# Attention scores and RG-LRU gates on 128 partitions: low parts of keys and gate weights in planes of their own beside zeros

## The chip, the cores and the metric

The kernel runs on one core of one Trainium2 chip. A core has a matrix engine (TensorE, PE in the profile; its weight loads are the rows PEld), a vector engine (VectorE, DVE), a scalar engine (ScalarE, ACT), a general engine (GpSimd, POOL) and an engine that here issues DMAs (SyncE, SP). The metric is the device time of one execution in microseconds (us); lower is better. Before the change the median of three runs is 1901.01 us (1900.91 to 1902.4).

## The reference, cut to what matters

One layer of a hybrid decoder in float32: a SwiGLU feed-forward half step (FFN1), a token mixer, a second feed-forward half step (FFN2). It takes a prompt of 1024 tokens and 8 sequences of 4 sampled tokens, with a model width of 1024. In the mixer two groups run side by side on the same normalised input: a gated linear recurrence (RG-LRU), whose gates come from eight 64 x 64 blocks of weights, and attention over a window of 128 with 8 query heads of 64 on 2 key/value heads.

```python
# RG-LRU gates, xb in 8 blocks of 64 channels
r = sigmoid(einsum('btnc,ncd->btnd', xb, wa) + ba)
i = sigmoid(einsum('btnc,ncd->btnd', xb, wx) + bx)
# attention scores; head size 64, keys: the block of 128 before and its own
s = einsum('...qkgd,...jkd->...kgqj', q, k) * 64 ** -0.5
```

## The kernel before, in words

Features lie on partitions, tokens along the free axis. The tokens are two halves: A has prompt tokens 0 to 511; B has tokens 512 to 1023 and the 32 sampled ones (544 columns, as two products of 272). TensorE goes through FFN1(A), FFN1(B) with the mixer of A between its units, FFN2(A) with the mixer of B, and FFN2(B).

A float32 product is made of float32r products over an exact split of each operand: hi (rounded to float32r) and lo (the rest), as hi.hi + hi.lo + lo.hi. In the main line that is three products for each tile of 128 x 128 weights: `mm3` (L380, lines 381 to 383, 512 columns) for A and `mm3w` (L385, lines 391 and 392, 272 columns) for B.

Where the sum runs over only 64 features, one product takes two of the three parts at a time. The gates (`lru`, L726): of each tile of 128 channels, for each block v of 64, the input's hi lies on the block's 64 partitions and its lo on the other 64 (`ct`, lines 780 to 784). The hi of the gate weights lies on both halves (`lw[:, li, v]`), so one product over 128 partitions (line 791) gives hi.hi and hi.lo. The lo of the weights lies on the block's own 64 partitions of plane 2 of `lw`, and a second product on line 791, over those 64 partitions (`lw[o, li, 2]` and `ct[o]`), adds the third part to the same bank.

The scores (`attn`, L997; one generator for each block of 128 queries and key/value head v) are built alike: `qt` has the queries' hi on the head's own 64 partitions and the lo on the others. `kb`, filled by `keys` (L943), has the keys' hi of each head on both halves (planes 0 and 1) and the lo of both heads in plane 2, each on its own 64 partitions. For each of four queries' tiles one product over 128 partitions (line 1019) is followed by one over 64 (line 1020), both into the same bank; four products make one request to the planner, two requests a block. Scores are 256 columns wide, 128 in the first block of the prompt. The sampled tokens' scores (`attn_s`, L1087) use `mm3` over 128 partitions with the other head's queries set to zero; one of their three stretches of keys takes hi and lo from `kb` (line 1134).

The order of the work is written out by a planner at build time. Every step is a Python generator that asks for an engine with an estimated duration and what it depends on (`Req`); `Sched.run` always emits the instruction that can start first by the estimate. Each engine then executes its instructions in that order, waiting on semaphores. The positions of the mixer's units between those of the FFN stand in `POS`. The charge for four score products is 0.44 us, the charge for a gate product `dP(g, 2)`.

Behind the scores come a masked maximum on DVE (line 1025), the exponential on ACT (line 1037), a division on ACT or DVE (helper `copy`, lines 288 to 292), PE transposes (line 1057), the split of the probabilities (helper `copy` and line 1067) and the products with V (lines 1075, 1076). Other hand-overs to PE: the split of the queries (line 1006) and that of the weight units, which come in by DMA (line 339), go through ACT (line 359) and DVE (line 361) and have three places. `constants` (L660) sets up ones, identity and the like on POOL at the start.

Of the kernel before, what the change touches and what calls it, by code (L numbers as in the profile page):

```python
"""One layer (macaron SwiGLU FFN, RG-LRU + windowed attention mixer, macaron SwiGLU FFN) for a
1024-token prompt and 8 x 4 sampled tokens, run as two halves: tokens 0-511 of the prompt (A), then
tokens 512-1023 with the 32 sampled ones (B). The tensor engine goes through FFN1(A), FFN1(B) with the
mixer of A, FFN2(A) with the mixer of B, FFN2(B).

Features lie on partitions and tokens along the free axis. A float32 product runs as three float32r
passes over exact splits (hi = rounded to float32r, lo = the rest): hi.hi + hi.lo + lo.hi.
"""
# [9 lines left out]
F32 = mybir.dt.float32  # L18
# [7 lines left out]
NB, NT = 8, 4                 # sampled sequences, tokens of each  # L26
T = SEQ + NB * NT             # 1056
HALF = 512                    # prompt tokens of a half
T0, TW = (0, HALF), (HALF, T - HALF)
CB = TW[1] // 2               # columns of a product of B  # L30
# [6 lines left out]
DOWN = {3: 0, **{g[0]: n + 1 for n, g in enumerate(GROUPS[2:])}}     # after which tile of h a group's products come  # L37
NEG = -1e30

# columns of the small per-partition operands  # L40
# [8 lines left out]
N_FFN = 2 * NF + 4 * 5 + 2    # weight units of one FFN  # L49
U_IN = N_FFN                  # k, v, q 0-3, x 0-3, gate 0-3  # L50
# [5 lines left out]
# where the units of the mixer stand between those of the FFN that runs beside it  # L56
POS = ({"k": 19, "v": 21, "q": (5, 5, 27, 28), "x": (6, 8, 12, 24), "g": (28, 30, 33, 36), "o": (47, 48, 48, 49, 49, 49, 50, 52)},
       {"k": 14, "v": 5, "q": (9, 11, 11, 11), "x": (6, 6, 16, 19), "g": (21, 26, 42, 45), "o": (57, 57, 57, 57, 57, 59, 59, 60)})
# of the estimate: reluctance to change the ACT tables, their change, and what an instruction of ACT or DVE has besides its columns
PEN, LOAD, EXTRA = 2.0, 2.6, {"A": 0.12, "D": 0.09}  # L60
WARM = 10                     # products of zeros that raise the tensor engine's clock before the first operands come
ORDER = ((0, 1, 2, 3), (0, 1, 2, 3, "s"))     # of the blocks of attention in A and B; "s": the sampled tokens
MODES = (None, "tanh", "tanh")     # how FFN1(B) and FFN2(A) take silu
MAINCAP = 6                   # banks that products of the main line may hold
DBIAS = 0.8                   # against the vector engine, where the scalar engine can do the same


class Tok:
    """The end of an instruction, by the estimate that orders the emission; None until it is emitted."""
# [6 lines left out]
class Req:  # L76
    __slots__ = ("eng", "dur", "deps", "sets", "when", "lat", "bias")

    def __init__(self, eng, dur, *deps, sets=None, when=None, lat=0.15, bias=0.0):
        self.eng, self.dur, self.deps, self.sets, self.when, self.lat = eng, dur, deps, sets, when, lat  # L80
        self.bias = bias      # against this one of several engines


class Sched:
    """Orders the emission: of all generators' next instructions, the one that can start first."""
# [60 lines left out]
class Banks:  # L146
    """The 8 banks of PSUM, alone or in pairs."""
# [32 lines left out]
class Pool:  # L180
    """Places in an arena, each with the end of its last use."""
# [26 lines left out]
def layer(ctx: ExitStack, tc, t):  # L208
# [15 lines left out]
    kb = const.tile([128, 3, WIN + W], F32R, name="kb")           # hi of each head, lo; the block before the half, then the half  # L224
    vt = const.tile([128, 5, 4, 64], F32R, name="vt")             # the block before the half, then the half; hi and lo of head 0, lo and hi of 1
# [3 lines left out]
    lw = const.tile([128, NLW, 3, 128], F32R, name="lw")          # hi of each block on both halves of the partitions, lo  # L229
    cols = const.tile([128, NCOL], F32, name="cols")  # L230
    ones = const.tile([128, 128], F32R, name="ones")
    bd1 = const.tile([128, 128], F32R, name="bd1")                # ones in each head's block
# [4 lines left out]
    xc3 = const.tile([128, 4, 3], F32, name="xc3")                # the end of A, for B  # L237
# [4 lines left out]
    qss = const.tile([128, 5, 4, 2], F32, name="qss")             # queries' 1 / rms: block (the sampled ones last), head  # L242
# [18 lines left out]
    def P_(b, g):  # L261
        """The product of a half in PSUM: one bank for A, two for B."""
        return ps[:, b:b + 2, :CB] if g else ps[:, b, :]

    def S_(ap, g):
        """A half in SBUF, in the form of P_."""
        return ap.rearrange("p (c n) -> p c n", c=2) if g else ap
# [13 lines left out]
    def dual(n, *deps, psum=False, when=None):  # L281
        """Requests for one pass over n columns on ACT or on DVE."""
        return (Req("A", 0.1 + n * 0.83e-3, *deps, when=when),
                Req("D", 0.07 + n * (1.04e-3 if psum else 0.52e-3), *deps, when=when, bias=DBIAS))

# [13 lines left out]
    tok = Toks()              # named ends: what another generator waits for  # L299
# [4 lines left out]
    def column_sums(lhs, x, g, tk):  # L304
        """lhs (of ones) times x, by x's hi and lo; returns the bank."""
# [16 lines left out]
    order = []                # the units as the main line takes them  # L322
# [3 lines left out]
    FIRST = 2                 # units that come and are split in pieces between the tiles of x; two more wait in the places of B's x  # L326
# [46 lines left out]
    def wait(n, k0):  # L373
        """The weights of unit n from k-tile k0 on."""
        return tok["w", n, k0 * len(pieces_of(n)) // KD]
# [9 lines left out]
    def mm3w(b, g, wh, wl, ah, al, first, last):  # L385
        """The three passes for a half."""
# [9 lines left out]
    def group(n, j, g, srcs, deps):  # L396
        """One [128 features, half] product; srcs: (hi, lo) of the k-tiles; the weights are tile j of unit n."""
# [18 lines left out]
    def abreast(parts):  # L416
        """Products side by side; their results."""
# [33 lines left out]
    def mean_rsqrt(xs, deps, g, n, out, acc, sq, sq2):  # L451
        """out = rsqrt(mean of squares + eps) of the feature tiles xs."""
# [12 lines left out]
    X = [list(range(KD)), list(range(KD, 2 * KD))]        # the places of x  # L465
# [4 lines left out]
    def xsplit(st, name, g):  # L470
        """x with the norm's gain into hi and lo; the products are divided by the rms."""
# [15 lines left out]
    def prenorm(st, name, g):  # L487
        """x / rms with the norm's gain into hi and lo."""
# [22 lines left out]
    def ffn(st, g, st2, u0, mode, rslot=None):  # L511
        """Steps of one FFN on a half: (generator, weight units). mode: "late" divides the products by the rms."""
# [3 lines left out]
        def evg(b, tk, f):  # L516
# [14 lines left out]
            else:             # silu(z) = z (1 + tanh(z / 2)) / 2  # L531
# [49 lines left out]
        def down(gi, m0, mp):  # L581
# [10 lines left out]
            if gi == len(GROUPS) - 1 and m0 == 0:  # L592
                # side by side, while the newest h is still on its way
# [27 lines left out]
    # ================= start =================  # L621
# [7 lines left out]
    def start():  # L629
        """The first loads, in the order in which the products take them."""  # L630
# [29 lines left out]
    def constants():  # L660
# [5 lines left out]
        G.memset(qss, 1.0)  # L666
        yield Req("Q", 0.6, Tok(60.0))
        SP.dma_start(mask, t["mask"])
        # softplus(-lambda), from tanh and the series of atanh
# [42 lines left out]
    # ================= the mixer =================  # L712
# [13 lines left out]
    def lru(i, g, xp):  # L726
# [18 lines left out]
        # convolution  # L745
# [20 lines left out]
        for v in range(2):  # L766
# [6 lines left out]
            V.tensor_tensor(lw[o, li, 2], raw[o], f32(lw[o, li, v]), OP.subtract)  # L773
        # gates: of each block of 64 channels both, from hi and lo on the two halves of the partitions
# [3 lines left out]
        for v in range(2):  # L778
# [10 lines left out]
            for w_, a_, st_ in ((lw[:, li, v], ct, True), (lw[o, li, 2], ct[o], False)):  # L789
                for c in range(1 + g):  # L790
                    PE.matmul(ps[:, b + c, :n], w_, a_[:, c * n:(c + 1) * n], start=st_, stop=not st_)  # L791
# [9 lines left out]
        # a = exp(-8 softplus(-lambda) r); 1 - a^2 = (1 + a^2) tanh(8 softplus(-lambda) r)  # L801
# [9 lines left out]
        # z ** 0.5 = z y, y = z ** -0.5 from exp(-ln(z) / 2) and one step of Newton  # L811
# [17 lines left out]
        if g:  # L829
            # h0 enters the first token of a sampled sequence, whose decay is then cut  # L830
# [60 lines left out]
    def query(b, tk, j, g):  # L891
        """Gain and rotary; the rms divides the scores."""
# [50 lines left out]
    def keys(s, g):  # L943
        """The keys: hi of each head on both halves of the partitions, lo of both heads on their own."""
# [6 lines left out]
        lo = kb[:, 2, WIN:WIN + TW[g]]  # L951
        for v in range(2):
            hi = kb[:, v, WIN:WIN + TW[g]]
# [43 lines left out]
    def attn(g, b, v, ri, Ps, mi):  # L997
# [3 lines left out]
        qt = rm[:, ri, :512]          # hi on the head's own partitions, lo on the others  # L1001
# [5 lines left out]
        whole = g or b                # the block before counts  # L1007
# [5 lines left out]
        kh, kl = kb[:, v, ks], kb[o, 2, ks]  # L1013
        for jj in (0, 2):
            tk = yield Req("P", 0.44, tk, tok["KB", g], banks.soon(), when=banks.has())
            bk = banks.get()
            for j in (jj, jj + 1):
                out = ps[:, bk, (j - jj) * 256 + ko:(j - jj + 1) * 256]
                PE.matmul(out, qt[:, j * 128:j * 128 + 128], kh, start=True, stop=False)  # L1019
                PE.matmul(out, qt[o, j * 128:j * 128 + 128], kl, start=False, stop=True)  # L1020
# [57 lines left out]
        # the parts with lo of V lie on the other partitions  # L1078
# [457 lines left out]
```

## Time and profile before

| what | value |
|---|---|
| median of three runs | 1901.01 us |
| span of the profiled execution, first to last instruction | 1898.9 us |
| granted TensorE clock, mean | 1.000 |
| DVE, ACT busy | 56%, 42% of the span |
| DMA queue q1, share of 16 engines | 29.6% |

The profile has no separate time for the profiled execution beyond its span; the median of the runs lies 2.1 us above that span. A row of a timeline has the start (us from the start of the span), the duration (us), engine, line, operation, the tile written and those read, and sizes: `128*128 128x256` is a product over 128 partitions into 128 rows, with 256 columns moving; `64*128` is one over 64 partitions. `x2` is a merged row of two. A group's row ends with the count, busy time, mean of one (ns), and the idle time ahead of it with what ended it. A row of the waits names who waited for whom, the total (us), how often, and the longest. A row of an instruction by line has minimum, median and maximum of its duration (ns), then first and last start. A row of windows has, for a stretch, its length, then the busy time and instructions of PE, PEld, DVE, ACT and POOL, the granted clock, the DMA share and GB/s. PE products are pipelined, so their rows overlap.

### The profile page before, as it was taken

How to read it: one execution, taken by the hardware profiler on the slowest of the kernel's cores; microseconds unless marked ns; L12 is line 12 of the kernel's file. 1: busy time of each engine (PE TensorE's matmuls, PEld its weight loads, DVE VectorE, ACT ScalarE, POOL GpSimd, SP SyncE). 2: the span in 40 equal slices, each digit the busy share in tenths (PEclk: the TensorE clock that was granted, in tenths of full speed). 3: DMA queues.
4: the chain of work that ended last, by engine and by line, in shares of the span. 5: the costliest groups of instructions: out<-in, count | busy, mean ns of one | idle time of the engine just before them, and what ended most of it. 6: DMA issues, size and time to landing. Idle time of an engine off the chain costs nothing.

```text
span 1898.9 us, 27922 instructions
## 1 busy us (share of the span) xinstructions
PE 1892.9 (100%) x11634; PEld 1702.3 (90%) x11634; DVE 1065.3 (56%) x1638; ACT 790.7 (42%) x1176; POOL 10.3 (1%) x35
## 2 busy tenths in 40 slices
PE   9999999999999999999999999999999999999999
PEld 7888888899999889989988988778889899999999
DVE  6774444476665767646576766766654643233333
ACT  5342222244645466424456566563543322222221
POOL 0000000000000000000000000000000000000000
PEclk9999999999999999999999999999999999999999
DMA  5422223243222212322242322223332322222222
GB/s 168 141 98 92 97 94 117 92 145 99 82 92 96 83 57 74 127 100 87 82 152 94 106 90 78 80 75 103 113 113 90 133 89 89 89 90 90 89 88 82
DMA packets 60253, 187.97 MB, mean 99 GB/s; under 512 B 7376, under 2 KB 9936, under 8 KB 60112
## 3 DMA queue, kind: packets, MB, share of 16 engines
q1 hardware_dynamic: 59984, 186.09, 29.6%
q8 instruction: 91, 1.49, 0.3%
q14 instruction: 34, 0.28, 0.0%
q10 hardware_dynamic: 144, 0.10, 0.0%
HBM read 174.58 MB, written 9.90 MB: 97 GB/s over the span
## 4 chain that ended last, share of the span: by engine, by line
PE 99%; DVE 0%; DMA 0%; ACT 0%; SPq 0%; issue 0%; ACTq 0%
PE ps L391 25%; PE ps L392 24%; PE ps L381 15%; PE ps L382 15%; PE ps L383 15%; PE ps L1020 1%; PE ps L1019 1%; PE ps L1057 1%; PE ps L791 1%; PE ps L1075 0%; PE ps L1076 0%; PE ps L907 0%; PE ps L317 0%; DMA fa<-x 0%; PE ps L1183 0%; DVE fa L556 0%
## 5 line engine op out<-in xcount | busy, mean ns | idle before, releaser
L359 ACT ACTIVATE whi<-raw 128x1024 fp32r<-128x1024 f32 (+1 forms) x312 | 325.2, 1042 | 707.2 <-issue 270.1
L361 DVE TENSOR_TENSOR wlo<-raw,whi 128x1024 fp32r<-128x1024 f32 (+1 forms) x312 | 375.4, 1203 | 195.6 <-ACT whi L359 189.6
L381 PE MATMUL ps<-xh,whi 128*128 128x512 f32 x880 | 350.6, 398 | 0.1
L382 PE MATMUL ps<-xl,whi 128*128 128x512 f32 x880 | 347.6, 395 | 0.3 <-DVE xl L476 0.3
L383 PE MATMUL ps<-xh,wlo 128*128 128x512 f32 x880 | 347.4, 395 | 0.0
L391 PE MATMUL ps<-xh,whi 128*128 128x272 f32 x880 | 256.7, 292 | 0.0
L391 PE MATMUL ps<-xl,whi 128*128 128x272 f32 x880 | 254.0, 289 | 0.0
L392 PE MATMUL ps<-xh,whi 128*128 128x272 f32 x880 | 253.7, 288 | 0.0
L392 PE MATMUL ps<-xl,whi 128*128 128x272 f32 x880 | 253.1, 288 | 0.0
L391 PE MATMUL ps<-xh,wlo 128*128 128x272 f32 x880 | 252.6, 287 | 0.0
L392 PE MATMUL ps<-xh,wlo 128*128 128x272 f32 x880 | 252.6, 287 | 0.0
L556 DVE SCALAR_TENSOR_TENSOR fa<-ps,fa 128x512 f32<-128x512 f32 (+1 forms) x192 | 135.6, 707 | 172.0 <-PE ps L392 103.5
L381 PEld LDWEIGHTS ps<-xh,whi 128*128 128x128 f32 x880 | 165.8, 188 | 38.9 <-ACT xh L474 0.9
L383 PEld LDWEIGHTS ps<-xh,wlo 128*128 128x128 f32 x880 | 165.8, 188 | 38.6
L382 PEld LDWEIGHTS ps<-xl,whi 128*128 128x128 f32 x880 | 165.9, 189 | 37.0 <-DVE xl L476 1.1
L391 PE MATMUL ps<-ha,whi 128*128 128x272 f32 x704 | 191.5, 291 | 0.0
L392 PE MATMUL ps<-ha,whi 128*128 128x272 f32 x704 | 190.8, 288 | 0.0
L391 PEld LDWEIGHTS ps<-xh,whi 128*128 128x128 f32 x880 | 165.4, 188 | 3.5 <-issue 1.5
L392 PEld LDWEIGHTS ps<-xh,whi 128*128 128x128 f32 x880 | 166.3, 189 | 1.3
L392 PEld LDWEIGHTS ps<-xl,whi 128*128 128x128 f32 x880 | 166.5, 189 | 0.0
L391 PEld LDWEIGHTS ps<-xh,wlo 128*128 128x128 f32 x880 | 165.9, 189 | 0.0
L392 PEld LDWEIGHTS ps<-xh,wlo 128*128 128x128 f32 x880 | 165.9, 188 | 0.0
(236 smaller groups left out, 2738.9 us busy)
## 6 DMA issues: line engine op xcount, KB each, us to landing
raw<-w SPq DMA_DIRECT2D x304, 512.0 KB, 3.3
fa<-x SPq DMA_DIRECT2D x8, 272.0 KB, 3.9
xs<-fa SPq DMA_DIRECT2D x8, 272.0 KB, 5.6
fa<-xs SPq DMA_DIRECT2D x8, 272.0 KB, 2.9
y<-fa SPq DMA_DIRECT2D x8, 272.0 KB, 2.0
fa<-x SPq DMA_DIRECT2D x8, 256.0 KB, 4.5
xs<-fa SPq DMA_DIRECT2D x8, 256.0 KB, 4.6
fa<-xs SPq DMA_DIRECT2D x8, 256.0 KB, 3.5
```

The lines of the kernel that those rows point to most:

```text
L359: S.activation(hi, raw, AF.Copy)
L361: V.tensor_tensor(lo, raw, f32(hi), OP.subtract)
L381: PE.matmul(p, wh, ah, start=first, stop=False)
L382: PE.matmul(p, wh, al, start=False, stop=False)
L383: PE.matmul(p, wl, ah, start=False, stop=last)
L391: PE.matmul(ps[:, b, :CB], w, a[:, c0], start=s, stop=e)
L392: PE.matmul(ps[:, b + 1, :CB], w, a[:, c1], start=s, stop=e)
L556: V.scalar_tensor_tensor(x, P_(b, g), fac, x, op0=OP.mult, op1=OP.add)
L791: PE.matmul(ps[:, b + c, :n], w_, a_[:, c * n:(c + 1) * n], start=st_, stop=not st_)
L1019: PE.matmul(out, qt[:, j * 128:j * 128 + 128], kh, start=True, stop=False)
L1020: PE.matmul(out, qt[o, j * 128:j * 128 + 128], kl, start=False, stop=True)
L1057: PE.transpose(ps[:, bk, j * 128:(j + 1) * 128], P[j // 2][:, j % 2, hf * 128:(hf + 1) * 128], ident)
```

## The change

The tile `kb` gets a fourth plane and `lw` too. The lo of head 0's keys stays in plane 2, that of head 1 goes to plane 3; in each plane the other 64 partitions are set to zero once, at the start, by GpSimd. The gate weights' lo of block 0 and 1 lie in planes 2 and 3 of `lw` in the same way. The second product of each pair then runs over all 128 partitions: the lo of the keys or weights meets the hi on its own partitions, and zeros meet the lo on the others. The sampled tokens' scores read plane 2 + v. The program's `dynamic_dma_scratch_size` is set to 1024. The rest of the diff takes out comments.

```diff
-    kb = const.tile([128, 3, WIN + W], F32R, name="kb")
+    kb = const.tile([128, 4, WIN + W], F32R, name="kb")
-    lw = const.tile([128, NLW, 3, 128], F32R, name="lw")
+    lw = const.tile([128, NLW, 4, 128], F32R, name="lw")
...
         G.memset(qss, 1.0)
+        for v in range(2):
+            u = slice(64 - 64 * v, 128 - 64 * v)
+            G.memset(f32(kb[u, 2 + v]), 0.0)
+            G.memset(f32(lw[u, :, 2 + v]), 0.0)
...
-            V.tensor_tensor(lw[o, li, 2], raw[o], f32(lw[o, li, v]), OP.subtract)
+            V.tensor_tensor(lw[o, li, 2 + v], raw[o], f32(lw[o, li, v]), OP.subtract)
...
-            for w_, a_, st_ in ((lw[:, li, v], ct, True), (lw[o, li, 2], ct[o], False)):
+            for w_, st_ in ((lw[:, li, v], True), (lw[:, li, 2 + v], False)):
                 for c in range(1 + g):
-                    PE.matmul(ps[:, b + c, :n], w_, a_[:, c * n:(c + 1) * n], start=st_, stop=not st_)
+                    PE.matmul(ps[:, b + c, :n], w_, ct[:, c * n:(c + 1) * n], start=st_, stop=not st_)
...
-        lo = kb[:, 2, WIN:WIN + TW[g]]
         for v in range(2):
-            hi = kb[:, v, WIN:WIN + TW[g]]
+            hi, lo = kb[:, v, WIN:WIN + TW[g]], kb[:, 2 + v, WIN:WIN + TW[g]]
...
-        kh, kl = kb[:, v, ks], kb[o, 2, ks]
+        kh, kl = kb[:, v, ks], kb[:, 2 + v, ks]
...
-                PE.matmul(out, qt[o, j * 128:j * 128 + 128], kl, start=False, stop=True)
+                PE.matmul(out, qt[:, j * 128:j * 128 + 128], kl, start=False, stop=True)
...
-                kh, kl = (kb[:, v, WIN + HALF:], kb[:, 2, WIN + HALF:]) if h == 2 else (krh, krl)
+                kh, kl = (kb[:, v, WIN + HALF:], kb[:, 2 + v, WIN + HALF:]) if h == 2 else (krh, krl)
...
-    nc = _bacc.Bacc("TRN2", target_bir_lowering=False, num_devices=1)
+    nc = _bacc.Bacc("TRN2", target_bir_lowering=False, num_devices=1, dynamic_dma_scratch_size=1024)
```

## The prediction

> **What bounds the kernel now.** I read four views: the page (engines, chain of waits), the waits of TensorE, the timelines of PE and PEld around one attention block, and the instructions of the lines that the change touches.
>
> ```profile
> span 1898.9 us, 27922 instructions
> PE 1892.9 (100%) x11634; PEld 1702.3 (90%) x11634; DVE 1065.3 (56%) x1638; ACT 790.7 (42%) x1176; POOL 10.3 (1%) x35
> PE 99%; DVE 0%; DMA 0%; ACT 0%; SPq 0%; issue 0%; ACTq 0%
> PE ps L652 <- DVE rm L650: 1.6, 1, 1.6
> PE ps L382 <- DVE xl L476: 0.3, 1, 0.3
> ```
>
> PE is busy for the whole span and is 99% of the chain that ended last. In the whole run it waits 1.9 us for another engine, all of it in the first microseconds. So the time is the sum of what PE's products occupy, and only what shortens PE's own stream counts. But a busy row is not a row at its peak: rows overlap, so the cost of a product is the distance from its start to the start of the next one. That distance must be read from a timeline. Here is PE in one attention block (eight score products), with the main stream before and behind it:
>
> ```profile
> 1204.67 0.39 PE L383 MATMUL ps<-ha,wlo 128*128 128x512 f32 x1
> 1204.90 0.28 PE L1019 MATMUL ps<-kb,rm 128*128 128x256 f32 x1
> 1205.11 0.38 PE L1020 MATMUL ps<-kb,rm 64*128 64x256 f32 x1
> 1205.43 0.38 PE L1019 MATMUL ps<-kb,rm 128*128 128x256 f32 x1
> ...
> 1207.30 0.50 PE L381 MATMUL ps<-ha,whi 128*128 128x512 f32 x1
> 1207.63 0.39 PE L382 MATMUL ps<-ha,whi 128*128 128x512 f32 x1
> ```
>
> In the main stream a 512-column product takes 0.23 us (1204.67 to 1204.90). Inside the block, where products on 128 and on 64 partitions alternate, a 256-column product takes 0.31 us (1205.11 to 1205.43), longer than one with twice the columns. The first product back on 128 partitions, L381 at 1207.30, again takes 0.33. The weight loads (PEld) in the same stretch say why:
>
> ```profile
> 1204.68 0.19 PEld L1019 LDWEIGHTS ps<-kb,rm 128*128 128x128 f32 x1
> 1205.11 0.18 PEld L1020 LDWEIGHTS ps<-kb,rm 64*128 64x128 f32 x1 [0.25 <-issue]
> 1207.30 0.19 PEld L381 LDWEIGHTS ps<-ha,whi 128*128 128x128 f32 x1
> 1207.40 0.19 PEld L382 LDWEIGHTS ps<-ha,whi 128*128 128x128 f32 x1
> ```
>
> The first score's weights load at 1204.68, under the product before it, 0.22 ahead of its own product. L1020's weights start only at 1205.11, together with their product, after PEld had stood 0.25 us with nothing to wait for. The load back to 128 partitions (1207.30) starts with its product too, and the next load follows 0.10 later. [...]
>
> **The change part by part.** It removes the 64-partition form from two places; each instruction there stays, on 128 partitions. The counts:
>
> ```profile
> L1019 PE MATMUL ps<-kb,rm x64: 220/382/388, 642.0 to 1248.4; 128*128 128x256 f32 x56, 128*128 128x128 f32 x8
> L1020 PE MATMUL ps<-kb,rm x64: 322/382/384, 642.1 to 1248.8; 64*128 64x256 f32 x56, 64*128 64x128 f32 x8
> L791 PE MATMUL ps<-rm,lw x48: 282/338/504, 460.9 to 1152.4; 128*128 128x272 f32 x16, 64*128 64x272 f32 x16, 128*128 128x512 f32 x8, 64*128 64x512 f32 x8
> ```
>
> For a 256-column product with its own load among products of full height, the trace has the sampled tokens' products:
>
> ```profile
> 1323.38 0.28 PE L381 MATMUL ps<-rm 128*128 128x256 f32 x1
> 1323.50 0.28 PE L382 MATMUL ps<-rm 128*128 128x256 f32 x1
> 1289.00 0.26 PE L383 MATMUL ps<-kb,rm 128*128 128x32 f32 x1
> 1289.11 0.26 PE L381 MATMUL ps<-kb,rm 128*128 128x32 f32 x1
> ```
>
> So 0.12 us for 256 columns (1323.38 to 1323.50), and 0.11 for a 32-column one, where the load sets the pace; I take 0.11 for 128 columns, between the two.
>
> *Scores, 256 columns.* Before: 1204.90 to 1207.63 is 2.73 us for eight scores and one 512-column product. After: 8 x 0.12 + 0.23 = 1.19. Saved 1.54 a block; 56 pairs at four a block are 14 blocks: **21.6 us**.
>
> *Scores, 128 columns* (the first prompt block, where the block before doesn't count), and the gates:
>
> ```profile
> 641.98 0.22 PE L1019 MATMUL ps<-kb,rm 128*128 128x128 f32 x1
> 644.25 0.39 PE L382 MATMUL ps<-xl,whi 128*128 128x512 f32 x1
> 460.63 0.29 PE L391 MATMUL ps<-xh,wlo 128*128 128x272 f32 x1
> 460.75 0.29 PE L392 MATMUL ps<-xh,wlo 128*128 128x272 f32 x1
> 460.88 0.82 PE L791 MATMUL ps<-rm,lw 128*128 128x512 f32 x2
> 461.86 0.29 PE L392 MATMUL ps<-xh,whi 128*128 128x272 f32 x1
> 1149.58 0.85 PE L791 MATMUL ps<-rm,lw 128*128 128x272 f32 x4
> 1150.70 0.39 PE L382 MATMUL ps<-xl,whi 128*128 128x512 f32 x1
> ```
>
> The score group runs from 641.98 to 644.25, 2.27 us for eight scores and one product of 512; after, 8 x 0.11 + 0.23 = 1.11. Saved 1.16, twice: **2.3 us**. A gate group of half A (two products of 512, then the first one of 272 behind them) takes 460.88 to 461.86, 0.98; after, 2 x 0.23 + 0.125 (460.63 to 460.88 is two of 272) = 0.585: 0.395 saved. A group of half B (four of 272, one of 512 behind) takes 1.12; after, 0.73: 0.39 saved. The counts give eight groups of each half: **6.3 us**. PE's stream becomes 30.2 us shorter.
>
> The removed form is the only new unknown: that these very operands stream at 0.12 when full. Bounds: 0.31 (nothing gained) and 0.11 (the pace of the loads, 1289.00 to 1289.11). I take 0.12, since the 32-column rows above read `kb` and `rm` too and pace at 0.11.
>
> [...]
>
> *What is added.* Four POOL memsets of zeros at the start, and 128 more columns in one ACT copy of the last keys.
>
> ```profile
> L662 POOL MEMSET bd<- 128x128 f32 x1 | 0.2, 204 | 0.3 <-POOLq L1525 0.3
> L664 POOL MEMSET bd<- 64x64 f32 x1 | 0.1, 146 | 0.0
> L949 ACT ACTIVATE kb<-kb x1: 508/508/508, 1087.6 to 1087.6; 128x384 fp32r<-128x384 f32 x1
> L976 PE MATMUL ps<-ident,fa x8: 271/273/273, 567.6 to 983.1; 128*128 128x128 f32 x8
> ```
>
> 64 columns more cost POOL 58 ns, so 672 columns are some 0.7 us and 128 some 0.2: 1.8 us for the four. Queued behind them on POOL is the identity, first used by PE at 567.6, so they are hidden. [...] The ACT copy is a third longer, 0.17 us, once, in a queue that is 42% busy: 0. The low parts are written by as many instructions of the same size into other planes: 0. No request of the planner changes, neither duration nor dependency, so the order on PE, DVE, ACT and SP stays, and no DMA is added. The smaller scratch of the DMA generator is not used by any queue that the page lists: 0.
>
> *What may be late next.* PE gets ahead of DVE and ACT where they hand work to it between scores. The tight places that I found by pairing producers with their products in order:
>
> ```profile
> 747.56 0.69 DVE L1067 TENSOR_TENSOR rm<-ps,rm 128x512 fp32r<-128x512 f32 x1
> 748.50 0.47 PE L1075 MATMUL ps<-rm,vt 128*128 128x512 f32 x1
> 675.07 0.61 DVE L292 TENSOR_SCALAR fa<-fa,mxt 128x256 f32<-128x256 f32 x2
> 676.55 0.49 PE L1057 MATMUL ps<-ident,fa 128*128 128x128 f32 x3
> 640.00:760.00 120.00, 120.00 (x793) 107.59 (x792) 83.55 (x204) 74.11 (x163) 0.00 (x0) 1.00 0.21 66
> ```
>
> The first pair leaves 0.25 us (748.25 to 748.50). The second leaves 0.87 (its two copies end at 675.68, the transposes begin at 676.55). Half a block saves 0.77. Of 62 such hand-overs (16 of queries, 16 of probabilities, 30 ahead of the products with V) I count seven between 0.25 and about 1, so PE could lose 0 to 7 x 0.77 = 5.4 us in new waits. DVE is busy for 83.6 and ACT for 74.1 of these 120 us, and their work comes earlier when PE does, so I take 1.5, near the low end.
>
> Sum: 30.2 - 1.5 = 28.7 us less. The profiled span of 1898.9 becomes 1870.2; the median of the runs lies 2.1 above the span (1901.0), so the time becomes **1872.3 us**.
>
> **The rivals.** (a) *The waits eat a good part.* In the attention stretches the chain through DVE and ACT doesn't shorten with PE. Each of 14 whole blocks keeps only a slack of about 0.87 of its 1.54 and loses 0.67: 9.4 us. Gain 20.8: 1880. For it: the slacks just shown. Against it: DVE and ACT are idle for 30% and more there, and the order was laid out with a charge of 0.44 us for four scores, while eight took 2.40 (1204.90 to 1207.30), 1.2 for four: it expects a faster PE than the trace has.
>
> (b) *Full-height loads are the exposed ones.* Then each of the 176 products (128 scores, 48 gates) shows its load of 0.10 (1207.30 to 1207.40): 18 us come back, gain 12: 1889. [...] Against it are 0.23 and 0.125 us a product throughout the main stream.
>
> (c) *No change.* It isn't the 64 partitions but these operands, or accumulating two products on one bank, that breaks the stream. Then 0.31 stays and 1901 with it. Against it: the products at 1323.38 and 1323.50 accumulate on one bank at 0.12, and L1019 itself starts at full pace at 1204.90.
>
> [...]
>
> **How the numbers follow.** Chances: forecast 76%, (a) 13%, (b) 3%, (c) 4%, (d) 4%. The forecast's own range is 1869 to 1877: without new waits and with 0.11 for the 112 wide scores (a further 1.1), and with all 5.4 of waits. The range goes on through (a) to 1882 at the high end; to 1868.5 at the low end, since runs differ by a microsecond. About 0.2%, 3.8 us, can be told from no change here: faster 92%, same 4%, slower 4%.
>
> **What would show it.** No `64*128` form is left at the lines of scores and gates; eight scores and the product behind take 1.2 us instead of 2.73, with each load ahead of its product; a gate group 0.59 and 0.73. TensorE's waits list stays under 7 us in all. The span loses 28 to 31, all of it between 460 and 1250. [...]

## The result and the profile after

The changed kernel takes 1858.7 us (median of four runs, 1858.59 to 1858.86) against 1901.0 before: 42.3 us less, a ratio of 0.9775 with a 95% interval of 0.9761 to 0.9789. The forecast was 1872.3 us, in a range of 1868.5 to 1882. The direction was right. The gain was half as large again as forecast, and the time lies below the range.

From the page of the changed kernel and from its list of TensorE's waits:

```profile
span 1856.5 us, 27927 instructions
PE 1850.5 (100%) x11634; PEld 1691.5 (91%) x11634; DVE 1064.3 (57%) x1638; ACT 790.4 (43%) x1176; POOL 12.3 (1%) x39
PE ps L652 <- DVE rm L650: 1.6, 1, 1.6
PE ps L381 <- ACT xh L474: 0.4, 1, 0.4
```

The span is 42.4 us shorter, and TensorE still works through all of it: the same 11,634 products, and waits of 2.0 us in all, as at the start of the run before. So the whole difference is in the pace of PE's own stream. The lines have moved: scores are now L1022 and L1023, gates L795. The timeline of PE around one attention block of the changed kernel:

```profile
1171.93 0.40 PE L383 MATMUL ps<-ha,wlo 128*128 128x512 f32 x1
1172.17 0.28 PE L1022 MATMUL ps<-kb,rm 128*128 128x256 f32 x1
1172.29 0.27 PE L1023 MATMUL ps<-kb,rm 128*128 128x256 f32 x1
...
1172.99 0.29 PE L1023 MATMUL ps<-kb,rm 128*128 128x256 f32 x1
1173.12 0.40 PE L381 MATMUL ps<-ha,whi 128*128 128x512 f32 x1
1173.36 0.39 PE L382 MATMUL ps<-ha,whi 128*128 128x512 f32 x1
```

Eight scores and the 512-column product behind them take 1.19 us (1172.17 to 1173.36); they took 2.73 before. The weight loads of the same stretch:

```profile
1171.93 0.19 PEld L1022 LDWEIGHTS ps<-kb,rm 128*128 128x128 f32 x1
1172.17 0.19 PEld L1023 LDWEIGHTS ps<-kb,rm 128*128 128x128 f32 x1
1173.00 0.19 PEld L381 LDWEIGHTS ps<-ha,whi 128*128 128x128 f32 x1
```

Each load now starts one product ahead of its own: L1023's load at 1172.17 for the product at 1172.29, and L381's at 1173.00 for 1173.12. No "issue" gap is left. The gate groups, on the same timeline:

```profile
455.10 0.62 PE L795 MATMUL ps<-rm,lw 128*128 128x512 f32 x2
455.56 0.29 PE L391 MATMUL ps<-xh,whi 128*128 128x272 f32 x1
455.69 0.29 PE L392 MATMUL ps<-xh,whi 128*128 128x272 f32 x1
...
1121.18 0.66 PE L795 MATMUL ps<-rm,lw 128*128 128x272 f32 x4
1121.68 0.40 PE L381 MATMUL ps<-xh,whi 128*128 128x512 f32 x1
1121.91 0.39 PE L382 MATMUL ps<-xl,whi 128*128 128x512 f32 x1
```

A group of half A takes 0.59 us (455.10 to 455.69) and one of half B 0.73 (1121.18 to 1121.91), where 0.585 and 0.73 were forecast.

But this timeline also shows what the forecast didn't have. The first gate product starts at 455.10, and before it started at 460.88. Ahead of it lies no product that the change touches: 5.8 us were gained in the main stream alone. From 150 to 340 us both kernels run nothing but 512-column products of half A's main stream. The view of windows counts PE's products in these 190 us, first before, then after (length, PE's busy time, count, clock, DMA share, GB/s):

```profile
150.00:340.00 190.00, 190.00 (x824) 1.00 0.30 101
```

```profile
150.00:340.00 190.00, 190.00 (x837) 1.00 0.31 101
```

The same clock, the same 101 GB/s, 13 products more. The page's group of the x tile's low part says which ones got shorter. Before:

```profile
L382 PE MATMUL ps<-xl,whi 128*128 128x512 f32 x880 | 347.6, 395 | 0.3 <-DVE xl L476 0.3
```

After:

```profile
L382 PE MATMUL ps<-xl,whi 128*128 128x512 f32 x880 | 342.8, 390 | 0.1
```

Same instruction, same shape, on average 5 ns less in each of 880. From here on I give the pace as the median distance from one product's start to the next one's, over all such pairs in the trace after 100 us: for this group 232 ns before and 227 after.

### The profile page after: what moved, and what is told of

Its sections match the earlier page's. It is cut to its first block, busy times and chain, and to the rows that moved or that the text cites. A ratio compares the mean times of both kernels' runs of the same rounds, so it can differ in the third digit from the quotient of the medians.

```text
span 1856.5 us, 27927 instructions
## 1 busy us (share of the span) xinstructions
PE 1850.5 (100%) x11634; PEld 1691.5 (91%) x11634; DVE 1064.3 (57%) x1638; ACT 790.4 (43%) x1176; POOL 12.3 (1%) x39
## 4 chain that ended last, share of the span: by engine, by line
PE 99%; DVE 0%; DMA 0%; ACT 0%; SPq 0%; issue 0%; ACTq 0%
PE ps L391 25%; PE ps L392 25%; PE ps L381 15%; PE ps L382 15%; PE ps L383 15%; PE ps L1060 1%; PE ps L795 0%; PE ps L1023 0%; PE ps L1022 0%; PE ps L1079 0%; PE ps L1078 0%; PE ps L911 0%; PE ps L317 0%; DMA fa<-x 0%; PE ps L1186 0%; DVE fa L556 0%
## 5 line engine op out<-in xcount | busy, mean ns | idle before, releaser
L381 PE MATMUL ps<-xh,whi 128*128 128x512 f32 x880 | 345.2, 392 | 0.4 <-ACT xh L474 0.4
L383 PE MATMUL ps<-xh,wlo 128*128 128x512 f32 x880 | 342.9, 390 | 0.0
L382 PE MATMUL ps<-xl,whi 128*128 128x512 f32 x880 | 342.8, 390 | 0.1
L381 PEld LDWEIGHTS ps<-xh,whi 128*128 128x128 f32 x880 | 165.4, 188 | 33.8 <-ACT xh L474 1.1
```

Source lines behind the costliest of these rows:

```text
L381: PE.matmul(p, wh, ah, start=first, stop=False)
L382: PE.matmul(p, wh, al, start=False, stop=False)
L383: PE.matmul(p, wl, ah, start=False, stop=last)
```

## What could have moved the main stream

The diff moves memory. The extra plane of `kb` is 672 columns of 4 bytes, 2688 = 10 x 256 + 128 bytes; it pushes the weight tiles `raw`, `whi` and `wlo` up against `xh`, `xl` and `ha`, which lie below. The scratch given up (16,384 to 1024) moves every tile down by 15,360 = 60 x 256. In the built programs the x tiles of half A start at 128 modulo 256 in both kernels; the weights start at 0 before and at 128 after. The theory that I tested: a 512-column product is faster where its moving operand and the weights lie equal modulo 256 bytes. The rivals: the smaller scratch or the absolute place does it, or the full rows do it all.

The trace before has a hint of this: its h products of equal shape did not run alike. On line 382 (low part of h, at 0 modulo 256, like the weights) the median was 226 ns, on line 381 (high part, at 128) 232. It was not the whole picture: line 383, which takes the high part too, stood at 228.

All ten experiments in one table. The place is that of the weights against the x tiles of half A, modulo 256 bytes; the pace is that of the xl products (median, ns); the count is that of PE's products from 150 to 340 us, all of 512 columns, from the view of windows. "Less than before" is taken against runs of the kernel before that were made beside each kernel (medians of 1900.7 to 1901.0 us). Runs of one kernel lie up to some 2 us apart, so a difference of medians and one of spans can disagree by about 1 us.

| kernel | median us | less than before | place | pace | count |
|---|---|---|---|---|---|
| before | 1900.8 | | 128 | 232 | 824 |
| after | 1858.7 | 42.3 | 0 | 227 | 837 |
| e1_scratch | 1900.8 | 0.0 | 128 | 232 | 824 |
| e2_rows_alone | 1871.9 | 28.9 | 128 | 232 | 824 |
| e3_weights_128 | 1889.5 | 11.3 | 0 | 227 | 838 |
| e4_after_back_128 | 1871.1 | 29.7 | 128 | 232 | 823 |
| e5_scores_alone | 1878.1 | 22.6 | 128 | 232 | 823 |
| e6_two_changes | 1889.0 | 11.7 | 128 | 232 | 824 |
| e7_x_128 | 1888.6 | 12.1 | 0 | 227 | 837 |
| e8_after_ha | 1857.1 | 43.6 | 0 | 227 | 840 |
| e9_h_by_half | 1854.5 | 46.4 | 0 | 227 | 840 |
| e10_after_64 | 1874.5 | 26.4 | 64 | 233 | 818 |

## The experiments

**The scratch alone.**

```diff
-    nc = _bacc.Bacc("TRN2", target_bir_lowering=False, num_devices=1)
+    nc = _bacc.Bacc("TRN2", target_bir_lowering=False, num_devices=1, dynamic_dma_scratch_size=1024)
```

> The kernel before with the smaller DMA scratch alone: every tile lies 15,360 bytes lower, all distances between tiles stay. After measured 1858.7, 42.3 us less than before, of which the products on 64 partitions explain about 30. Theory (the other 12 come from where the weights lie against the moving operand, modulo 256 bytes): nothing changes here, 1901 within 1.5 us. Rival (a smaller scratch or another absolute place makes it): 1889, and the main stream's 512-column products at 227 instead of 232 ns.

Measured 1900.8 us, a ratio of 1.0 (0.9991 to 1.001), and 824 products in the window, as before. Neither the smaller scratch nor a move of all tiles by 15,360 bytes changes anything.

**The full rows alone, every other tile at its old address.** The two new tiles stand first in the pool, in 3200 bytes that the scratch gives up.

```diff
+    kb3 = const.tile([128, WIN + W], F32R, name="kb3")
+    lw3 = const.tile([128, 128], F32R, name="lw3")
...
+    klo, wl = (kb[:, 2], kb3), (lw[:, 0, 2], lw3)
...
-        kh, kl = kb[:, v, ks], kb[o, 2, ks]
+        kh, kl = kb[:, v, ks], klo[v][:, ks]
...
+            S.activation(kb3[:, :WIN], f32(kb3[:, HALF:HALF + WIN]), AF.Copy)
```

> All products on 128 partitions as after, but the two added planes lie in space that the scratch gives up, so that every other tile lies at its address of before (the added copy of the keys' last block is a second ACT instruction). Theory (two separate gains): 1870.8, that is 30.2 us less and no new waits; the main stream's 512-column products stay at 232 ns. Rival (the whole gain comes from the full rows): 1859.

Measured 1871.9 us, ratio 0.9849 (0.9834 to 0.9864). The window of this kernel:

```profile
150.00:340.00 190.00, 190.00 (x824) 1.00 0.30 100
```

The main stream has its pace of before. By the spans the full rows are worth 30.0 us (1898.9 to 1868.9), by the medians 28.9; the forecast's sum was 30.2.

**128 bytes, and the 64-partition products kept.**

```diff
+    pad = const.tile([128, 32], F32, name="pad")
     vt = const.tile([128, 5, 4, 64], F32R, name="vt")
```

> The kernel before, products on 64 partitions as before, with 128 unused bytes ahead of the weights: raw, hi and lo of the weights lie 128 bytes higher, x and h where they were. Theory (places modulo 256 bytes): the 512-column products of the x tiles go from 232 to 227 ns, time 1889 (12 us less). Rival (the larger move of the tiles, or the smaller scratch, matters): 1901.

Measured 1889.5 us, ratio 0.9941 (0.9927 to 0.9956), and in the window:

```profile
150.00:340.00 190.00, 190.00 (x838) 1.00 0.31 103
```

An unused tile of 128 bytes ahead of the weights, in the kernel before, is worth 11.3 us. The x products go from 232 to 227 ns.

**The same 128 bytes put into the kernel after**, in the same place.

> The kernel after with 128 unused bytes ahead of the weights: they lie at multiples of 256 again, as before. Theory: the 12 us are lost again, 1871; the 512-column products of the x tiles back at 232 ns. Rival: 1859, as after.

Measured 1871.1 us, ratio 0.9845 (0.983 to 0.9859): 12.4 us of the gain are gone, and what is left is e2's. So the change's gain has two parts that add up: by the spans 30.0 (e2) and 12.6 (1869.1 to 1856.5), together 42.6, against 42.4 measured.

**The x tiles moved by 128 bytes, the weights by 256.**

```diff
+    pad = const.tile([128, 32], F32, name="pad")
     xh = [const.tile([128, KD, TW[g]], F32R, name=f"xh{g}") for g in range(2)]
...
+    pad2 = const.tile([128, 32], F32, name="pad2")
     kb = const.tile([128, 3, WIN + W], F32R, name="kb")
```

> The kernel before with the two x tiles (high and low) 128 bytes higher and the weights 256 bytes higher, so at the same place modulo 256; h stays. Theory (what counts is whether moving operand and weights lie equal modulo 256 bytes): the 512-column x products go from 232 to 227 ns, 12 us or a little more, 1888. Rival (it is the weights' own place that counts): 1901.

Measured 1888.6 us, ratio 0.9937 (0.9922 to 0.9952), pace 227 ns. The weights lie at 0 modulo 256 as in the kernel before, and the x products are fast all the same: for them it is the two operands' places against each other that count.

**Weights 64 bytes further, in the kernel after.**

```diff
+    pad = const.tile([128, 16], F32, name="pad")
     vt = const.tile([128, 5, 4, 64], F32R, name="vt")
```

> The kernel after with 64 unused bytes ahead of the weights, so that they lie 64 bytes off the moving operand modulo 256 for x of half A (after: 0; before: 128). Theory (only equal places modulo 256 are fast): 232 ns for the 512-column x products, 1871 for half A's part, with up to 3 us either way from half B. Rival (128 off is the one bad place): 227 and 1859.

Measured 1874.5 us, ratio 0.9858 (0.9841 to 0.9874), pace 233 ns. 64 bytes off are as slow as 128 (232 ns in e4): of the three places tried only the equal one is fast. The time is 3.4 us above e4's, more than I had worked out for the x products. Summed over the traces, the distances behind half A's products are 4.6 us longer than in e4, 2.5 in x and 2.1 in h (the mean of its h products is 231.7 ns here and 229.7 in e4), and those of half B 0.8 shorter. In e4 the low part of h still lay equal to the weights; here neither part does.

**Scores on 128 partitions, gates left on 64.** This is the kernel of e2 with one line changed:

```diff
-            for w_, a_, st_ in ((lw[:, li, v], ct, True), (wl[v], ct, False)):
+            for w_, a_, st_ in ((lw[:, li, v], ct, True), (wl[v][o], ct[o], False)):
```

> As e2_rows_alone, but only the scores run on 128 partitions, the gates' second product stays on 64. Theory: 23.9 us less than before (21.6 + 2.3), 1877; the gates' 6.3 stay lost against e2_rows_alone (1871.9). Rival (all of the gain hangs on fewer changes of height anywhere, or the gates cost nothing since they are few): under 1873.

Measured 1878.1 us, ratio 0.9881 (0.9865 to 0.9898): 22.6 us for the scores where 23.9 were worked out (by the spans 24.0: 1898.9 to 1874.9), and 6.1 more with the gates, where it was 6.3.

**Fewer changes of height, no zero planes.** The kernel before with the second tile of each pair in the order low, high:

```diff
-                PE.matmul(out, qt[:, j * 128:j * 128 + 128], kh, start=True, stop=False)
-                PE.matmul(out, qt[o, j * 128:j * 128 + 128], kl, start=False, stop=True)
+                pair = [(slice(0, 128), kh), (o, kl)]
+                for i, (rows, keys_) in enumerate(pair if j == jj else pair[::-1]):
+                    PE.matmul(out, qt[rows, j * 128:j * 128 + 128], keys_, start=i == 0, stop=i == 1)
```

> The kernel before, with the second score tile of each pair in the other order: high, low, low, high, so that two products on 64 partitions follow each other and a group of four has two changes of height, not four. Same products, no zero planes. Theory (each change of height costs, equal neighbours hide their loads): half of the scores' 23.9 us is saved, 12 less, 1889. Rival (it is each load on 64 partitions that isn't hidden, also behind another one on 64): 0.1 us for each of 28 wide groups and four narrow ones comes back, 3 us, so 1892. Rival (the changes cost nothing, zeros or other data matter): 1901.

Measured 1889.0 us, ratio 0.9937 (0.9922 to 0.9951). Eight scores on this kernel's timeline of PE (its scores are all on L1021; the merged row shows the first one's shape, half of them are on 64 partitions):

```profile
1196.64 0.39 PE L383 MATMUL ps<-ha,wlo 128*128 128x512 f32 x1
1196.87 1.89 PE L1021 MATMUL ps<-kb,rm 128*128 128x256 f32 x8
1198.60 0.40 PE L381 MATMUL ps<-ha,whi 128*128 128x512 f32 x1
1198.84 0.39 PE L382 MATMUL ps<-ha,whi 128*128 128x512 f32 x1
```

The same products, half of them still on 64 partitions, take 1.73 us (1196.87 to 1198.60) instead of 2.40. Half the changes of height, half the loss: 11.7 us against 12 expected. Two 64-partition loads in a row, and the product of the second, in the same stretch:

```profile
1197.08 0.18 PEld L1021 LDWEIGHTS ps<-kb,rm 64*128 64x128 f32 x1 [0.25 <-issue]
1197.19 0.19 PEld L1021 LDWEIGHTS ps<-kb,rm 64*128 64x128 f32 x1
...
1197.31 0.28 PE L1021 MATMUL ps<-kb,rm 64*128 64x256 f32 x1
```

The first load, at the change, has the same gap of 0.25 us ahead of it as in the kernel before; the second starts 0.12 us ahead of its product. So it is the change that costs, and a load on 64 partitions behind another one on 64 is hidden. Each change costs 0.19 us: the 23.9 us worked out, over 128 changes, two for each of the 64 score pairs; this kernel has 64 changes fewer and saves 11.7 us, 0.18 each. Why a change costs this is not shown.

**h moved too.** In the kernel after, the high part of an h tile lies equal to the weights and the low part, 544 columns behind, at 128 off. By the theory as I had put it, line 382 alone should be slow there. But the medians on lines 381, 382 and 383 are 235, 234 and 230 ns, and those on line 381 fall into two groups, near 227 and near 235. Where the places are mixed, then, a product's own place does not settle its pace. What was tried is to make them all equal. First with 576 columns:

```diff
-    ha = const.tile([128, NH, 2, W], F32R, name="ha")
+    ha = const.tile([128, NH, 2, 576], F32R, name="ha")
```

> The kernel after with rows of h padded from 544 to 576 columns, so that high and low parts of every h tile lie equal to the weights modulo 256 bytes, not only the high ones. Theory: the down products of half A (three products 232.4, 233.8 and 229.1 ns) come to 228 each, some 10 ns for each of 352 triples, 3.7 us less than after: 1855. Rival (h differs from x, place doesn't matter there): 1858.7.

Measured 1857.1 us, ratio 0.9769 (0.9754 to 0.9784): 1.6 us less than after, not 3.7. The mean of half A's h products fell from 231.8 to 227.8 ns, as expected, and the three lines stand at 227, 226 and 227. That of half B's rose from 125.6 to 126.6, which over some 2100 of them gives 2.1 us back. I had left half B out. It takes two products of 272 columns, whose second one starts 64 bytes off the first one's place in any case. So, by half:

```diff
-    ha = const.tile([128, NH, 2, W], F32R, name="ha")
+    ha = const.tile([128, NH, 1152], F32R, name="ha")
...
-            hh, hl = (ha[:, H[f], i, :TW[g]] for i in range(2))
+            hh, hl = (ha[:, H[f], i * (544 if g else 576):][:, :TW[g]] for i in range(2))
...
```

> The kernel after, with the low part of an h tile 576 columns behind the high one for half A and 544 for half B (in e8 576 for both gained 4 us in A's down products and lost 2 in B's, 126.6 against 125.6 ns). Theory: A keeps its gain, B its time of after: 1854.7, 4 us less than after. Rival (e8's loss in B doesn't hang on the place of the low part): 1857, as e8.

Measured 1854.5 us (1854.35 to 1854.68), ratio 0.9755 (0.9741 to 0.9770), 4.2 us below the kernel after, whose runs lie at 1858.59 to 1858.86. It leaves nothing out and is the fastest kernel of the study.

## Why the prediction was right and wrong, point by point

- *PE's stream is the time.* Right: waits 1.9 us before, 2.0 after, and every experiment's gain is a sum of distances between products.
- *The load is exposed where the height changes.* The price and the exposed load are right; e6 shows them without any zero plane (0.18 us a change, and 0.25 us idle ahead of the load). What lies behind the price is not shown. The sum of 30.2 us measured 30.0 by the spans, and its parts 24.0 and 6.0 (1874.9 to 1868.9) against 23.9 and 6.3; by the medians it measured 28.9, and its parts 22.6 and 6.1.
- *1.5 us of new waits.* Mis-sized: there were none. The hand-overs that I counted as tight did not turn into waits: the smallest slack between a split on DVE and its product with V is 0.25 us in both traces. DVE had room as well: ahead of its masked maximum it stood idle for TensorE for 29.2 us before (L1025) and for 12.6 after (L1028):

```profile
  PE ps L1020: 29.2, 22
...
  PE ps L1023: 12.6, 12
```

- *Rival (a), the waits eat a good part; (b), full-height loads are the exposed ones; (c), no change.* None came. (b) is contradicted by the trace after: a full-height load behind a full-height one starts under the product before (L1023's at 1172.17, 0.12 us ahead of its own product), and the loads that stood exposed in the trace before were those where the heights differed (L1020's at 1205.11, L381's at 1207.30, each with its product). Nor did the slower time come that got 4% under (d): the four runs took 1858.59 to 1858.86 us, each at a granted clock of 1.00.
- *What is added costs nothing.* The four memsets took 1.7 us on POOL in all, as sized, but they stand behind the identity there, not ahead of it as I wrote:

```profile
L669 POOL MEMSET kb<- 64x672 f32 x2 | 1.3, 652 | 0.1
L670 POOL MEMSET lw<- 64x128 f32 x2 | 0.4, 198 | 0.0
```

- **The step that failed** is in the same paragraph: the low parts go "into other planes: 0", and the smaller scratch is "0". I costed the new plane by the instructions that fill and read it, and not by the tiles that it pushes along. The scratch was indeed 0 (e1). The plane, 2688 bytes and so 128 modulo 256, was worth 12.4 us (e4 against after), all of it in products that the diff doesn't touch: between these two traces the scores and gates agree within 0.1 us. With the 1.5 us of waits that did not come, it makes up the distance from the 28.7 us that were forecast to the 42.3 measured, within 0.3. The forecast took the main stream's pace from the trace as given, and no bound was set on it; the low end of the range, 1868.5, held no gain from there.

## What to carry to other kernels

Where TensorE is the bound, count the changes between products of different height: each costs 0.19 us here, and zeros that keep every product at full height took them out (e2, 28.9 us with the gates); an order that puts equal heights side by side took out half of those in the scores (e6, 11.7 us). A diff that adds or enlarges an SBUF tile can also move the tiles behind it, as the plane of 2688 bytes did here, worth 12.4 us; compare the pace of untouched products before giving the gain to the edit, and put the tiles back by padding to separate the two.

## What the runs showed of the hardware that I had not expected

The float32r products of 512 columns with x paced at 227 ns where the moving operand and the weights lay at equal places modulo 256 bytes, and at 232 to 233 ns where they lay 64 or 128 bytes apart (e3, e4, e7, e10). Moving either one does it (the weights in e3, x in e7, 227 ns both); moving both by the same amount does nothing (e1, 232). From e4 to after, the x products of half A give 13.2 us, 0.7% of this kernel; h of half A takes 2.0 more and h of half B 2.0 less, and the rest is small. The h products of half A were all fast where both their parts lay equal to the weights (227, 226 and 227 ns on the three lines in e8; e9); with one part equal and one 128 bytes off, products at the equal place were slow too in the kernel after (a median of 235 ns on line 381). So the rule is shown for stretches in which every product lies equal, not for a single product among others. Half B's products of 272 columns showed much less, means of 125.4 to 126.7 ns over all kernels for x and for h, and in no simple order of places.

Why 256 bytes stays open. In the built programs the x tiles and the weights of every fast kernel lie equal modulo 512 too; only the low part of h in e8 and e9 lay 256 off, and it was fast, at 226 and 227 ns. Whether it is the place of the product's own weights or of the next ones that counts, and whether other places of x behave like 64 and 128, was not tried and stays open too.
